# A fused add and layer norm on one core: other chunk sizes, lags and store queues for the last chunks

## Chip, core and metric

The kernel runs on one core of a Trainium2 chip. The metric is the time of one execution on the device in microseconds (us); the span of a profile is the time from the first to the last instruction on the core and is some 2 us shorter than that time.

## What is computed

```python
def reference(x, residual, gamma, beta, eps):      # x, residual: 16 x 1024 x 512 float32
    z = x + residual
    mean = np.mean(z, axis=-1, keepdims=True)
    var = np.var(z, axis=-1, keepdims=True)
    z_norm = (z - mean) / np.sqrt(var + eps)
    return (gamma * z_norm + beta).astype(np.float32)
```

There are 16,384 rows of 512 numbers. Each row is read twice (from `x` and from `residual`) and written once: 67 MB in, 34 MB out.

## The kernel before

The rows are cut into 128 *units* of 128 rows, one row per partition of the on-chip memory. A *chunk* is one or more units that are loaded with one transfer for `x` (tile `z`), one for `residual` (tile `r`), and stored with one. `_chunk_schedule` (line 16) makes the list of chunk sizes: two chunks of 1, then chunks of 4 as long as they fit (29 of them), a remainder of 2, and eight chunks of 1 at the end: 40 chunks.

What happens to a chunk, stage by stage:

- `s_load` (line 119): SyncE issues both loads (lines 128 and 131). For each unit TensorE multiplies `z` and `r` by the identity and adds both into one bank of its accumulator memory, `ps` (lines 137 and 138): this is the addition `x + residual`.
- `s_copy` (line 159): ScalarE copies `ps` back to `z` and sums each row on the way (line 164).
- `s_square` (line 172): ScalarE squares `z` into a scratch tile `junk` and sums the squares (line 178).
- `s_smalls` (line 185): VectorE makes mean and variance for all units of the chunk from these sums, with three instructions on 128 x (units) numbers (lines 191, 194, 195).
- `s_sqrt` (line 204): ScalarE takes the root of variance + eps (line 208).
- `s_recip` (line 216): VectorE inverts it (line 221) and computes `nbias`, -mean / std (line 222). Nothing in the path that is used here reads `nbias`.
- `s_ap1` (line 254): VectorE computes (z - mean) * gamma, one instruction of 128 x 512 for each unit (line 258).
- `s_ap2_store` (line 267): VectorE computes that times 1/std plus beta, again one instruction for each unit (line 271); then GpSimd issues the store of the whole chunk (line 279).

The tiles `z` and `r` have ten buffers each, every one as large as the largest chunk; `ps` has eight.

The stages of a chunk are emitted with lags. In iteration `i` of the loop at line 307, a stage with lag `l` is emitted for chunk `i - l`; the lags are 0 for the load, 1 for copy and square, 2 for the small statistics and the root, 3 for the reciprocal and for `s_ap1`, and 4 for `s_ap2_store`:

```python
    for i in range(n_chunks + max_lag):
        for lag, fn in stages:
            c = i - lag
            if 0 <= c < n_chunks:
                fn(c)
```

The kernel is written in a tile framework, which places all semaphore waits and, when the context closes, fixes the order of the instructions on each engine. The emission order gives the priority; it need not be the final order. That order is fixed before the run[...].

Of the kernel before, what the change touches and what calls it, by code (L numbers as in the profile page):

```python
# [2 lines left out]

# [5 lines left out]


def _env(name, default):
    return int(os.environ.get(name, str(default)))


def _chunk_schedule(total_units, body_nj, head, tail):
    head = [h for h in head if h > 0]
    tail = [t for t in tail if t > 0]
    njs = []
    left = total_units - sum(head) - sum(tail)  # L20
    assert left >= 0
    njs += head
    n_body = left // body_nj
    njs += [body_nj] * n_body
    rem = left - n_body * body_nj
    if rem:
        njs += [rem]
    njs += tail
    assert sum(njs) == total_units
    return njs  # L30
# [3 lines left out]
def kernel(  # L34
# [6 lines left out]
    eps: bass.AP,  # L41
    out: bass.AP,
):
    USE_PE = _env("LN_PE", 1)
    NJ = _env("LN_NJ", 4)
    N_HEAD = _env("LN_HEAD", 2)
    N_TAIL = _env("LN_TAIL", 8)
    Z_BUFS = _env("LN_BUFS", 10)
    R_BUFS = _env("LN_RBUFS", 10)
    ST_BUFS = _env("LN_STBUFS", 8)  # L50
    PS_BUFS = _env("LN_PSBUFS", 8)
    OUT_Q = _env("LN_OUT_Q", 2)
    IN_Q = _env("LN_IN_Q", 0)
    L_CP = _env("LN_L_CP", 1)
    L_SQ = _env("LN_L_SQ", 1)
    L_SM = _env("LN_L_SM", 2)
    L_SQR = _env("LN_L_SQR", 2)
    L_RC = _env("LN_L_RC", 3)
    L_AF = _env("LN_L_AF", 3)
    L_GB = _env("LN_L_GB", 4)  # L60

    nc = tc.nc
    fp32 = mybir.dt.float32
# [11 lines left out]
    eps_f = float(eps)  # L75
    inv_d = 1.0 / float(D)

    assert N % P == 0
    total_units = N // P
    njs = _chunk_schedule(total_units, NJ, [1] * N_HEAD, [1] * N_TAIL)  # L80
    n_chunks = len(njs)
    starts = []
    row = 0
# [5 lines left out]
    def dview(t, c):  # L89
        nj = njs[c]  # L90
        return t[starts[c] : starts[c] + P * nj, :].rearrange(
            "(p j) d -> p (j d)", p=P
        )
# [2 lines left out]
    data = ctx.enter_context(tc.tile_pool(name="data", bufs=Z_BUFS))  # L96
    rpool = ctx.enter_context(tc.tile_pool(name="rpool", bufs=R_BUFS))
    stats = ctx.enter_context(tc.tile_pool(name="stats", bufs=ST_BUFS))
    if USE_PE:
        psum = ctx.enter_context(tc.tile_pool(name="psum", bufs=PS_BUFS, space=bass.MemoryType.PSUM))  # L100
        junkp = ctx.enter_context(tc.tile_pool(name="junkp", bufs=2))

    gamma_t = consts.tile([P, D], fp32)
    nc.gpsimd.dma_start(out=gamma_t, in_=gamma[None, :].to_broadcast((P, D)))  # L104
# [1 line left out]
    nc.gpsimd.dma_start(out=beta_t, in_=beta[None, :].to_broadcast((P, D)))  # L106
    eps_t = consts.tile([P, 1], fp32)
    nc.vector.memset(eps_t, eps_f)  # L108
    if USE_PE:
        ident = consts.tile([P, P], fp32)  # L110
        make_identity(nc, ident)
        junk = junkp.tile([P, D], fp32)

    in_q = {0: nc.sync, 1: nc.scalar, 2: nc.gpsimd}[IN_Q]
    out_q = {0: nc.sync, 1: nc.scalar, 2: nc.gpsimd}[OUT_Q]

    Z, R, PS, SUM, SSQ, MEAN, VAR, RSTD, NBIAS = {}, {}, {}, {}, {}, {}, {}, {}, {}

    def s_load(c):
        nj = njs[c]  # L120
        z = data.tile([P, NJB, D], fp32, tag="z")
        r = rpool.tile([P, NJB, D], fp32, tag="r")
        Z[c], R[c] = z, r
        sm = stats.tile([P, NJB], fp32, tag="sum")
        sq = stats.tile([P, NJB], fp32, tag="ssq")
        SUM[c], SSQ[c] = sm, sq
        if USE_PE:
            nc.sync.dma_start(  # L128
                out=z[:, :nj, :].rearrange("p a b -> p (a b)"), in_=dview(xf, c)
            )  # L130
            in_q.dma_start(  # L131
                out=r[:, :nj, :].rearrange("p a b -> p (a b)"), in_=dview(rf, c)
            )
            pss = []
            for j in range(nj):
                ps = psum.tile([P, D], fp32, tag="ps", name="ps")
                nc.tensor.matmul(ps, ident, z[:, j, :], start=True, stop=False)  # L137
                nc.tensor.matmul(ps, ident, r[:, j, :], start=False, stop=True)  # L138
                pss.append(ps)
            PS[c] = pss  # L140
        else:
            nc.sync.dma_start(
                out=z[:, :nj, :].rearrange("p a b -> p (a b)"), in_=dview(xf, c)
            )
            in_q.dma_start(
                out=r[:, :nj, :].rearrange("p a b -> p (a b)"), in_=dview(rf, c)
            )
            for j in range(nj):
                nc.vector.scalar_tensor_tensor(
                    out=z[:, j, :],  # L150
                    in0=z[:, j, :],
                    scalar=0.0,
                    in1=r[:, j, :],
                    op0=add,
                    op1=add,
                    accum_out=sm[:, j : j + 1],
                )

    def s_copy(c):
        nj = njs[c]  # L160
        z = Z[c]
        sm = SUM[c]
        for j in range(nj):
            nc.scalar.activation(  # L164
                out=z[:, j, :],
                in_=PS[c][j],
                func=mybir.ActivationFunctionType.Identity,
                accum_out=sm[:, j : j + 1],
            )
        PS.pop(c)  # L170

    def s_square(c):
        nj = njs[c]
        z, r = Z[c], R[c]
        sq = SSQ[c]
        dest = junk if USE_PE else r
        for j in range(nj):
            nc.scalar.activation(  # L178
                out=dest if USE_PE else r[:, j, :],
                in_=z[:, j, :],  # L180
                func=mybir.ActivationFunctionType.Square,
                accum_out=sq[:, j : j + 1],
            )

    def s_smalls(c):
        nj = njs[c]
        mean = stats.tile([P, NJB], fp32, tag="mean")
        var = stats.tile([P, NJB], fp32, tag="var")
        MEAN[c], VAR[c] = mean, var
        msq = var  # L190
        nc.vector.tensor_scalar(  # L191
            out=mean[:, :nj], in0=SUM[c][:, :nj], scalar1=inv_d, scalar2=None, op0=mult
        )
        nc.vector.tensor_mul(msq[:, :nj], mean[:, :nj], mean[:, :nj])  # L194
        nc.vector.scalar_tensor_tensor(  # L195
            out=var[:, :nj],
            in0=SSQ[c][:, :nj],
            scalar=inv_d,
            in1=msq[:, :nj],
            op0=mult,  # L200
            op1=sub,
        )
# [13 lines left out]
    def s_recip(c):  # L216
        nj = njs[c]
        rstd = RSTD[c]
        nbias = stats.tile([P, NJB], fp32, tag="nbias")
        NBIAS[c] = nbias  # L220
        nc.vector.reciprocal(out=rstd[:, :nj], in_=rstd[:, :nj])  # L221
        nc.vector.scalar_tensor_tensor(  # L222
            out=nbias[:, :nj],
            in0=MEAN[c][:, :nj],
            scalar=-1.0,
            in1=rstd[:, :nj],
            op0=mult,
            op1=mult,
        )

    def s_affine(c):
        nj = njs[c]
        z = Z[c]
        rstd, nbias = RSTD[c], NBIAS[c]
        for j in range(nj):
            nc.scalar.activation(
                out=z[:, j, :],
                in_=z[:, j, :],
                func=mybir.ActivationFunctionType.Identity,
                bias=nbias[:, j : j + 1],  # L240
                scale=rstd[:, j : j + 1],
            )

    def s_gb_store(c):
        nj = njs[c]
        z = Z[c]
        zb = z[:, :nj, :]
        nc.vector.tensor_mul(zb, zb, gamma_t[:, None, :].to_broadcast((P, nj, D)))
        nc.vector.tensor_add(zb, zb, beta_t[:, None, :].to_broadcast((P, nj, D)))
        out_q.dma_start(out=dview(of, c), in_=zb.rearrange("p a b -> p (a b)"))  # L250
        for dd in (Z, R, PS, SUM, SSQ, MEAN, VAR, RSTD, NBIAS):
            dd.pop(c, None)

    def s_ap1(c):
        nj = njs[c]
# [11 lines left out]
    def s_ap2_store(c):  # L267
        nj = njs[c]
        z, rstd = Z[c], RSTD[c]
        for j in range(nj):  # L270
            nc.vector.scalar_tensor_tensor(  # L271
                out=z[:, j, :],
                in0=z[:, j, :],
                scalar=rstd[:, j : j + 1],
                in1=beta_t,
                op0=mult,
                op1=add,
            )
        out_q.dma_start(  # L279
            out=dview(of, c),  # L280
            in_=z[:, :nj, :].rearrange("p a b -> p (a b)"),
        )
        for dd in (Z, R, PS, SUM, SSQ, MEAN, VAR, RSTD, NBIAS):
            dd.pop(c, None)

    stages = [(0, s_load)]
    if USE_PE:
        stages += [
            (L_CP, s_copy),
            (L_SQ, s_square),  # L290
            (L_SM, s_smalls),
# [2 lines left out]
            (L_AF, s_ap1),  # L294
            (L_GB, s_ap2_store),
        ]
    else:
        stages += [
            (L_SQ, s_square),
            (L_SM, s_smalls),  # L300
            (L_SQR, s_sqrt),
# [1 line left out]
            (L_AF, s_affine),  # L303
            (L_GB, s_gb_store),
        ]
    max_lag = max(l for l, _ in stages)
    for i in range(n_chunks + max_lag):
        for lag, fn in stages:
            c = i - lag
            if 0 <= c < n_chunks:  # L310
                fn(c)


# [33 lines left out]
```

## Time and profile before

| | |
|---|---|
| time, median of 4 runs | 254.98 us (254.38 to 256.59) |
| span of the profiled run | 252.8 us |
| TensorE matmul busy | 230.8 us (91%), 512 instructions |
| VectorE busy | 190.1 us (75%), 457 instructions |
| ScalarE busy | 191.8 us (76%), 554 instructions |
| GpSimd busy | 23.4 us (9%) |
| moved by DMA | 101.35 MB, mean 401 GB/s |

In the profile, PE is TensorE's matmul part and PEld its weight loading, DVE is VectorE, ACT is ScalarE, POOL is GpSimd and SP is SyncE (SPq its queue of issued transfers). A row of a timeline gives start, duration, engine, line of the kernel, operation, output and input, and in brackets the idle time before it with what ended it. The second part of the page cuts the span into 40 equal slices; each digit is a busy share in tenths. A busy share over the whole span is a mean over stretches with different limits, so the stretch in which the kernel ends has to be looked at by itself.

### The profile page before, as it was taken

The numbers are of one execution on the slowest core, as the hardware profiler recorded it, in microseconds if no ns is written. First come the engines' busy times: TensorE is split into PE (matmuls) and PEld (weight loads), VectorE is DVE, ScalarE is ACT, GpSimd is POOL, SyncE is SP. The second block draws the span as 40 slices with busy tenths as digits, with TensorE's granted clock in tenths as the row PEclk, the third lists the DMA queues.
The fourth block names the chain that finished last, engine by engine and source line by source line (L and its number), as shares of the span: only waits on it lengthen the run. The fifth ranks groups of instructions, "written<-read, shape, count | busy, mean of one in ns | idle before, by whom it ended". The sixth has DMA issues, their size and how long they took to land.

```text
span 252.8 us, 2444 instructions
## 1 busy us (share of the span) xinstructions
PE 230.8 (91%) x512; PEld 97.2 (38%) x512; DVE 190.1 (75%) x457; ACT 191.8 (76%) x554; POOL 23.4 (9%) x48
## 2 busy tenths in 40 slices
PE   4699999999999999899999999999999999999920
PEld 1134444444444443344333344343433443344400
DVE  0142888988888888788777779878777987779991
ACT  2357888888888888878878788787888878789860
POOL 3000000000000000000000000000000000000231
PEclk9959999999999999999999999999999999999985
DMA  6999999999999999999999999999999999999843
GB/s 183 388 428 424 425 421 426 423 426 430 423 428 425 426 428 425 426 425 424 425 428 425 426 425 428 423 425 429 423 425 428 426 428 423 413 406 392 348 162 124
DMA packets 16815, 101.35 MB, mean 401 GB/s; under 512 B 1952, under 2 KB 1952, under 8 KB 5664
## 3 DMA queue, kind: packets, MB, share of 16 engines
q1 hardware_dynamic: 11520, 67.11, 63.9%
q0 software_dynamic: 5280, 34.08, 32.8%
q8 instruction: 4, 0.07, 0.1%
q14 instruction: 11, 0.09, 0.1%
HBM read 67.63 MB, written 33.55 MB: 400 GB/s over the span
## 4 chain that ended last, share of the span: by engine, by line
DMA 78%; PE 13%; issue 4%; POOL 2%; SPq 1%; POOLq 0%
DMA r<-in_residual_dram 76%; PE ps L138 7%; PE ps L137 6%; DMA z<-in_x_dram 2%; POOL out_dram L279 2%; SPq L128 1%; SPq L131 0%; POOLq L342 0%; POOLq L279 0%
## 5 line engine op out<-in xcount | busy, mean ns | idle before, releaser
L138 PE MATMUL ps<-r,ident 128*128 128x512 f32 x256 | 134.9, 609 | 6.0 <-DMA r<-in_residual_dram 6.0
L137 PE MATMUL ps<-z,ident 128*128 128x512 f32 x256 | 134.4, 607 | 5.0 <-DMA z<-in_x_dram 4.9
L164 ACT ACTIVATE z<-ps 128x512 f32<-128x512 f32 x128 | 76.2, 595 | 32.1 <-PE ps L138 30.9
L258 DVE SCALAR_TENSOR_TENSOR z<-z,mean,gamma_t 128x512 f32<-128x512 f32 x128 | 94.3, 742 | 0.0
L271 DVE SCALAR_TENSOR_TENSOR z<-z,std,beta_t 128x512 f32<-128x512 f32 x128 | 88.4, 747 | 0.0
L178 ACT ACTIVATE junk<-z 128x512 f32<-128x512 f32 x128 | 80.8, 631 | 3.9
L138 PEld LDWEIGHTS ps<-r,ident 128*128 128x128 f32 x256 | 47.9, 193 | 76.0 <-issue 52.5
L137 PEld LDWEIGHTS ps<-z,ident 128*128 128x128 f32 x256 | 49.3, 194 | 67.9 <-issue 54.3
L191 DVE TENSOR_SCALAR mean<-sm 128x4 f32<-128x4 f32 (+2 forms) x40 | 6.6, 166 | 52.4 <-ACT z L164 52.4
L279 POOL DMA_DIRECT2D out_dram<-z x40 | 21.5, 536 | 223.9 <-DVE z L271 199.7
L164 ACT ACTIVATION_READ_ACCUMULATOR z<-ps 128x1 f32 x128 | 24.9, 195 | 0.0
L178 ACT ACTIVATION_READ_ACCUMULATOR junk<-z 128x1 f32 x128 | 24.0, 188 | 0.0
L208 ACT ACTIVATE std<-var,eps_t 128x4 f32<-128x4 f32 (+2 forms) x40 | 11.9, 297 | 14.4 <-DVE var L195 14.2
L221 DVE RECIPROCAL std<-std 128x4 f32<-128x4 f32 (+2 forms) x40 | 6.8, 169 | 2.9 <-ACT std L208 2.9
L194 DVE TENSOR_TENSOR var<-mean 128x4 f32<-128x4 f32 (+2 forms) x40 | 6.5, 161 | 1.1
L195 DVE SCALAR_TENSOR_TENSOR var<-sq,var 128x4 f32<-128x4 f32 (+2 forms) x40 | 6.3, 157 | 0.3 <-ACT junk L178 0.3
L222 DVE SCALAR_TENSOR_TENSOR nbias<-mean,std 128x4 f32<-128x4 f32 (+2 forms) x40 | 6.3, 158 | 0.1
L164 ACT ACT_TABLE_LOAD x1 | 1.3, 1283 | 3.4 <-DMA z<-in_x_dram 3.4
L208 ACT ACT_TABLE_LOAD x1 | 1.3, 1283 | 0.0
L104 POOL DMA_DIRECT2D gamma_t<-in_gamma_dram x1 | 0.7, 677 | 0.8 <-POOLq L328 0.8
L108 DVE MEMSET eps_t<- 128x1 f32 x1 | 0.1, 59 | 0.8 <-PEq L328 0.8
L106 POOL DMA_DIRECT2D beta_t<-in_beta_dram x1 | 0.5, 543 | 0.0
(6 smaller groups left out, 0.9 us busy)
## 6 DMA issues: line engine op xcount, KB each, us to landing
z<-in_x_dram SPq DMA_DIRECT2D x29, 1024.0 KB, 29.4
r<-in_residual_dram SPq DMA_DIRECT2D x29, 1024.0 KB, 29.5
out_dram<-z POOLq DMA_DIRECT2D x29, 1024.0 KB, 9.3
z<-in_x_dram SPq DMA_DIRECT2D x10, 256.0 KB, 7.9
r<-in_residual_dram SPq DMA_DIRECT2D x10, 256.0 KB, 8.0
out_dram<-z POOLq DMA_DIRECT2D x10, 256.0 KB, 2.4
z<-in_x_dram SPq DMA_DIRECT2D x1, 512.0 KB, 28.3
r<-in_residual_dram SPq DMA_DIRECT2D x1, 512.0 KB, 24.7
```

Of the source, the lines that this page charges most:

```text
L137: nc.tensor.matmul(ps, ident, z[:, j, :], start=True, stop=False)
L138: nc.tensor.matmul(ps, ident, r[:, j, :], start=False, stop=True)
L164: nc.scalar.activation(out=z[:, j, :], in_=PS[c][j], func=mybir.ActivationFunctionType.Identity, accum_out=sm[:, j : j + 1],)
L178: nc.scalar.activation(out=dest if USE_PE else r[:, j, :], in_=z[:, j, :], func=mybir.ActivationFunctionType.Square, accum_out=sq[:, j : j ...
L191: nc.vector.tensor_scalar(out=mean[:, :nj], in0=SUM[c][:, :nj], scalar1=inv_d, scalar2=None, op0=mult)
L194: nc.vector.tensor_mul(msq[:, :nj], mean[:, :nj], mean[:, :nj])
L195: nc.vector.scalar_tensor_tensor(out=var[:, :nj], in0=SSQ[c][:, :nj], scalar=inv_d, in1=msq[:, :nj], op0=mult, op1=sub,)
L208: nc.scalar.activation(out=std[:, :nj], in_=VAR[c][:, :nj], func=mybir.ActivationFunctionType.Sqrt, bias=eps_t[:, 0:1], scale=1.0,)
L221: nc.vector.reciprocal(out=rstd[:, :nj], in_=rstd[:, :nj])
L258: nc.vector.scalar_tensor_tensor(out=z[:, j, :], in0=z[:, j, :], scalar=mean[:, j : j + 1], in1=gamma_t, op0=sub, op1=mult,)
L271: nc.vector.scalar_tensor_tensor(out=z[:, j, :], in0=z[:, j, :], scalar=rstd[:, j : j + 1], in1=beta_t, op0=mult, op1=add,)
L279: out_q.dma_start(out=dview(of, c), in_=z[:, :nj, :].rearrange("p a b -> p (a b)"),)
```

## The change

Most of the diff tidies: constants in place of environment variables, a test on the row length in place of a flag, a `fast_path` function that always returns false, and `junk` in a pool of one buffer in place of two. Five parts change what runs:

- the chunk sizes: two of 1, 28 of 4, then 2, 2, 2, 2, 2, 2, 1, 1 (38 chunks); the aim is finer work near the end than chunks of 4, with fewer transfers than chunks of 1;
- `nbias` isn't computed any more on this path;
- `s_ap1` gets lag 4, where it had 3, so that both wide VectorE stages are emitted in the same iteration;
- the last six chunks get shorter lags, 3 for both wide stages, so that they are emitted sooner;
- the stores of the last four chunks are issued by SyncE, the others still by GpSimd.

```diff
 def _chunk_schedule(total_units, body_nj, n_head, n_tail):
+    head = [1] * min(n_head, total_units)
+    tail = [2, 2, 2, 2, 2, 2, 1, 1]
+    left = total_units - len(head) - sum(tail)
+    njs = list(head)
+    njs += [body_nj] * (left // body_nj)
...
+    DRAIN_FAST = 6
+    L_CP, L_SQ, L_SM, L_SQR, L_RC, L_AF, L_GB = 1, 1, 2, 2, 3, 4, 4
...
         nc.vector.reciprocal(out=rstd[:, :nj], in_=rstd[:, :nj])
-        nc.vector.scalar_tensor_tensor(
-            out=nbias[:, :nj],
-            in0=MEAN[c][:, :nj],
-            scalar=-1.0,
-            in1=rstd[:, :nj],
-            op0=mult,
-            op1=mult,
-        )
...
-        out_q.dma_start(
-            out=dview(of, c),
-            in_=z[:, :nj, :].rearrange("p a b -> p (a b)"),
+        (nc.sync if c >= n_chunks - 4 else nc.gpsimd).dma_start(
+            out=dview(of, c), in_=z[:, :nj, :].rearrange("p a b -> p (a b)")
         )
...
+        tail_lags = [0, 1, 1, 2, 2, 3, 3, 3]
...
-    max_lag = max(l for l, _ in stages)
-    for i in range(n_chunks + max_lag):
-        for lag, fn in stages:
-            c = i - lag
-            if 0 <= c < n_chunks:
-                fn(c)
+    emit = []
+    for c in range(n_chunks):
+        fast = c >= n_chunks - DRAIN_FAST
+        for si, (lag, _fn) in enumerate(stages):
+            emit.append((c + (tail_lags[si] if fast else lag), si, c))
+    emit.sort()
+    for _lvl, si, c in emit:
+        stages[si][1](c)
```

For chunks with the ordinary lags the sorted list gives the same order as the two loops did: by iteration, then by stage.

More of the change, by code (lines that the diff above doesn't have):

```diff
@@ L2 @@
-import os
 from contextlib import ExitStack
@@ L9, with _chunk_schedule @@
 from concourse.masks import make_identity
[L12 to L27, printed above, removed]
+def _chunk_schedule(total_units, body_nj, n_head, n_tail):
+    head = [1] * min(n_head, total_units)
[3 more added lines that the diff above has]
+    njs += [body_nj] * (left // body_nj)
+    if left % body_nj:
+        njs.append(left % body_nj)
     njs += tail
@@ L43 @@
 ):
[L44 to L60, printed above, removed]
+    NJ = 4
+    N_HEAD = 2
+    N_TAIL = 8
+    DRAIN_FAST = 6
+    Z_BUFS = 10
+    R_BUFS = 10
+    ST_BUFS = 8
+    PS_BUFS = 8
+    L_CP, L_SQ, L_SM, L_SQR, L_RC, L_AF, L_GB = 1, 1, 2, 2, 3, 4, 4
     nc = tc.nc
@@ L76 @@
     inv_d = 1.0 / float(D)
-    assert N % P == 0
+    assert N % P == 0, "row count must be a multiple of the partition count"
+    use_pe = D <= 512
     total_units = N // P
-    njs = _chunk_schedule(total_units, NJ, [1] * N_HEAD, [1] * N_TAIL)
+    njs = _chunk_schedule(total_units, NJ, N_HEAD, N_TAIL)
     n_chunks = len(njs)
@@ L98 @@
     stats = ctx.enter_context(tc.tile_pool(name="stats", bufs=ST_BUFS))
-    if USE_PE:
+    if use_pe:
         psum = ctx.enter_context(tc.tile_pool(name="psum", bufs=PS_BUFS, space=bass.MemoryType.PSUM))
-        junkp = ctx.enter_context(tc.tile_pool(name="junkp", bufs=2))
+        junkp = ctx.enter_context(tc.tile_pool(name="junkp", bufs=1))
     gamma_t = consts.tile([P, D], fp32)
@@ L108 @@
     nc.vector.memset(eps_t, eps_f)
-    if USE_PE:
+    if use_pe:
         ident = consts.tile([P, P], fp32)
@@ L112, with fast_path @@
         junk = junkp.tile([P, D], fp32)
-    in_q = {0: nc.sync, 1: nc.scalar, 2: nc.gpsimd}[IN_Q]
-    out_q = {0: nc.sync, 1: nc.scalar, 2: nc.gpsimd}[OUT_Q]
-    Z, R, PS, SUM, SSQ, MEAN, VAR, RSTD, NBIAS = {}, {}, {}, {}, {}, {}, {}, {}, {}
+    Z, R, PS, SUM, SSQ, MEAN, VAR, RSTD, NBIAS = ({} for _ in range(9))
+    def fast_path(c):
+        return False
     def s_load(c):
@@ L126, in s_load @@
         SUM[c], SSQ[c] = sm, sq
-        if USE_PE:
-            nc.sync.dma_start(
-                out=z[:, :nj, :].rearrange("p a b -> p (a b)"), in_=dview(xf, c)
-            )
-            in_q.dma_start(
-                out=r[:, :nj, :].rearrange("p a b -> p (a b)"), in_=dview(rf, c)
-            )
+        zv = z[:, :nj, :].rearrange("p a b -> p (a b)")
+        rv = r[:, :nj, :].rearrange("p a b -> p (a b)")
+        nc.sync.dma_start(out=zv, in_=dview(xf, c))
+        nc.sync.dma_start(out=rv, in_=dview(rf, c))
+        if use_pe and not fast_path(c):
             pss = []
@@ L141, in s_load @@
         else:
[L142 to L147, printed above, removed]
             for j in range(nj):
@@ L159, in s_copy @@
     def s_copy(c):
+        if fast_path(c):
+            return
         nj = njs[c]
-        z = Z[c]
-        sm = SUM[c]
+        z, sm = Z[c], SUM[c]
         for j in range(nj):
@@ L173, in s_square @@
         nj = njs[c]
-        z, r = Z[c], R[c]
-        sq = SSQ[c]
-        dest = junk if USE_PE else r
+        z, r, sq = Z[c], R[c], SSQ[c]
         for j in range(nj):
             nc.scalar.activation(
-                out=dest if USE_PE else r[:, j, :],
+                out=junk if (use_pe and not fast_path(c)) else r[:, j, :],
                 in_=z[:, j, :],
@@ L189, in s_smalls @@
         MEAN[c], VAR[c] = mean, var
-        msq = var
         nc.vector.tensor_scalar(
@@ L193, in s_smalls @@
         )
-        nc.vector.tensor_mul(msq[:, :nj], mean[:, :nj], mean[:, :nj])
+        nc.vector.tensor_mul(var[:, :nj], mean[:, :nj], mean[:, :nj])
         nc.vector.scalar_tensor_tensor(
@@ L198, in s_smalls @@
             scalar=inv_d,
-            in1=msq[:, :nj],
+            in1=var[:, :nj],
             op0=mult,
@@ L218, in s_recip @@
         rstd = RSTD[c]
-        nbias = stats.tile([P, NJB], fp32, tag="nbias")
-        NBIAS[c] = nbias
         nc.vector.reciprocal(out=rstd[:, :nj], in_=rstd[:, :nj])
-        nc.vector.scalar_tensor_tensor(
-            out=nbias[:, :nj],
-            in0=MEAN[c][:, :nj],
-            scalar=-1.0,
-            in1=rstd[:, :nj],
-            op0=mult,
-            op1=mult,
[L229 to L241, printed above, removed]
-            )
[L244 to L252, printed above, removed]
+        if not use_pe:
+            nbias = stats.tile([P, NJB], fp32, tag="nbias")
+            NBIAS[c] = nbias
+            nc.vector.scalar_tensor_tensor(
+                out=nbias[:, :nj],
+                in0=MEAN[c][:, :nj],
+                scalar=-1.0,
+                in1=rstd[:, :nj],
+                op0=mult,
+                op1=mult,
+            )
     def s_ap1(c):
@@ L284, in s_ap2_store, with s_affine, s_gb_store @@
             dd.pop(c, None)
-    stages = [(0, s_load)]
-    if USE_PE:
-        stages += [
+    def s_affine(c):
+        nj = njs[c]
+        z = Z[c]
+        rstd, nbias = RSTD[c], NBIAS[c]
+        for j in range(nj):
+            nc.scalar.activation(
+                out=z[:, j, :],
+                in_=z[:, j, :],
+                func=mybir.ActivationFunctionType.Identity,
+                bias=nbias[:, j : j + 1],
+                scale=rstd[:, j : j + 1],
+            )
+    def s_gb_store(c):
+        nj = njs[c]
+        zb = Z[c][:, :nj, :]
+        nc.vector.tensor_mul(zb, zb, gamma_t[:, None, :].to_broadcast((P, nj, D)))
+        nc.vector.tensor_add(zb, zb, beta_t[:, None, :].to_broadcast((P, nj, D)))
+        nc.gpsimd.dma_start(out=dview(of, c), in_=zb.rearrange("p a b -> p (a b)"))
+        for dd in (Z, R, PS, SUM, SSQ, MEAN, VAR, RSTD, NBIAS):
+            dd.pop(c, None)
+    if use_pe:
+        stages = [
+            (0, s_load),
             (L_CP, s_copy),
@@ L296 @@
         ]
+        tail_lags = [0, 1, 1, 2, 2, 3, 3, 3]
     else:
-        stages += [
+        stages = [
+            (0, s_load),
             (L_SQ, s_square),
@@ L305 @@
         ]
-    max_lag = max(l for l, _ in stages)
-    for i in range(n_chunks + max_lag):
-        for lag, fn in stages:
-            c = i - lag
-            if 0 <= c < n_chunks:
-                fn(c)
+        tail_lags = [0, 1, 2, 2, 3, 3, 4]
+    emit = []
[6 more added lines that the diff above has]
+        stages[si][1](c)
 _INS = ['x', 'residual', 'gamma', 'beta', 'eps']
```

## The prediction

> **What bounds the kernel now.** I read the slices of the page first, then the stretches, then the timeline of the end. Units are 128 rows; there are 128 of them.
>
> ```profile
> DVE  0142888988888888788777779878777987779991
> DMA  6999999999999999999999999999999999999843
> GB/s 183 388 428 424 425 421 426 423 426 430 423 428 425 426 428 425 426 425 424 425 428 425 426 425 428 423 425 429 423 425 428 426 428 423 413 406 392 348 162 124
> ```
>
> One slice is 6.32 us. For 32 slices the DMA engines are full at about 425 GB/s with VectorE at 7 to 8 tenths; in the last three the rate falls to 348, 162, 124 and VectorE stands at 9, 9, 9. So the body is bound by transfers and the end by something else. The stretches say what.
>
> ```profile
> 100.00:200.00 100.00, 96.01 (x217) 39.96 (x216) 79.55 (x178) 79.72 (x230) 6.93 (x13) 1.00 1.01 426
> 218.00:225.40 7.40, 7.07 (x18) 3.17 (x18) 5.83 (x13) 5.92 (x17) 0.53 (x1) 1.00 1.03 406
> 234.00:242.00 8.00, 7.85 (x19) 3.19 (x17) 8.00 (x33) 6.93 (x22) 2.17 (x4) 1.00 0.78 312
> 242.00:247.60 5.60, 0.00 (x0) 0.00 (x0) 5.56 (x21) 2.26 (x8) 2.10 (x4) 0.69 0.44 168
> ```
>
> The columns are PE, PEld, DVE, ACT, POOL busy, clock, DMA share, GB/s. Until 225 VectorE has slack; from 234 to 247.6 it has none (8.00 of 8.00, 5.56 of 5.60), while DMA is at 0.78 and then 0.44. The timeline of VectorE shows where this begins and ends:
>
> ```profile
> 217.98 0.17 DVE L191 TENSOR_SCALAR mean<-sm 128x4 f32<-128x4 f32 x1 [1.50 <-ACT z L164]
> 218.27 0.75 DVE L258 SCALAR_TENSOR_TENSOR z<-z,mean,gamma_t 128x512 f32<-128x512 f32 x1
> 221.13 2.73 DVE L271 SCALAR_TENSOR_TENSOR z<-z,std,beta_t 128x512 f32<-128x512 f32 x4
> 225.44 0.17 DVE L191 TENSOR_SCALAR mean<-sm 128x4 f32<-128x4 f32 x1 [1.58 <-ACT z L164]
> ...
> 246.80 0.76 DVE L271 SCALAR_TENSOR_TENSOR z<-z,std,beta_t 128x512 f32<-128x512 f32 x1
> 247.12 0.54 POOL L279 DMA_DIRECT2D out_dram<-z  x1 [0.98 <-DVE z L271]
> 247.85 0.54 POOL L279 DMA_DIRECT2D out_dram<-z  x1 [0.19 <-issue]
> ```
>
> Two chunks of four units start at 217.98 and 225.44. After the first, VectorE is done at 223.86 and idles 1.58 us, because the mean of a chunk needs the copies of all four units. From 225.44 it never stops until 247.56. That is the path: a late start by a coarse chunk, then 22.12 us of VectorE for the last 14 units, then the store.
>
> The timeline also shows that the emitted order is not the order on the engine: the first multiply (L258) of a chunk follows its mean (L191) at once, though the loop emits it an iteration later. The builder moves ready work into VectorE's idle time; lags matter only where VectorE is short.
>
> **What the Trainium skill says.** "Perfetto Trace Analysis", Optimization Strategy: the most contended engine can change over time within a kernel, and is to be judged by regime. The trace agrees (DMA share 1.01 from 100 to 200, VectorE 5.56 of 5.60 us at the end). "VectorE: DVE Perf Modes", Rules for kernel authors: keep the number of operations small, since each flushes the pipe. The trace shows a small price for independent ones: 241.90, 241.97, 242.04, 242.10 are starts of four in a row, 0.07 us apart, and 242.10 to 242.76 makes a wide one 0.66. "DMA: Bandwidth & Descriptors", Issuing engines are not separate DMA queues: another issuing engine brings no bandwidth, only issue time. The page agrees so far: SyncE's loads and GpSimd's stores take 63.9 and 32.8% of one set of 16 engines, 96.7% together. Same page, Latency and other measured facts: first byte about 0.6 us for a transfer issued by SyncE against about 1 us by GpSimd. No SyncE store is in this trace.
>
> **The change part by part.**
>
> *Price check.* By these prices the 22.12 us from 225.44 are 28 wide (28 x 0.66 = 18.48) and 10 chunks of 5 small (50 x 0.07 = 3.50): 21.98.
>
> *Chunks.* The last 14 units, before one of 4, one of 2 and eight of 1, become six of 2 and two of 1; units 2 to 113 stay in fours. So the first line of the fence stays at 217.98, and the next mean needs two copies, not four. Units 114 and 115 pass PE by about 217.06 + 4 x 0.86 = 220.5 and their copies end before 222, before VectorE is free at 223.9. The idle 1.58 us go.
>
> *One small operation fewer* (line 222, which nothing uses here): before, 5 per chunk and 11 chunks from 217.98; after, 4 per chunk and 9 chunks. 55 - 36 = 19 x 0.07 = 1.3 us less. In the body the same removal costs and gives nothing: there VectorE has 1.5 us idle in each 7.4, under transfers.
>
> *Sum on VectorE after:* 36 wide x 0.66 = 23.76, 36 small x 0.07 = 2.52, 0.3 for the first dependent pair (217.98 to 218.19 instead of 0.07) and the last one's full length: 26.6, to 244.6 instead of 247.56.
>
> *Other floors.* PE: at 217.06 two matmuls of 0.43 end at 217.92, the next starts at 218.41 because the residual of the 4-unit chunk is late. With half the size it is there: 0.49 earlier, so PE ends at 241.36 instead of 241.85. Then copy 0.70, square 0.78, variance 0.20, root 0.35, reciprocal 0.21, wide 0.75, hand-overs 0.1: 3.1, to 244.5. DMA: the stretches from 218 to 250 sum to 10.4 MB; at 406 GB/s 25.5 us, to 243.5. Do earlier stores starve the loads? A 1 MB store lands in 9.2 us beside loads, thus takes some 114 GB/s, and stores are in flight from 216.8 to 233 before too; the loads keep their pace and end near 235, PE wants the last at 239.6.
>
> *Three floors within 1.1 us* won't be met exactly: I add 0.6, one wait of the root for its variance (0.51 at 238.73) and a hand-over. Bounds 0 and 2.0, the latter if the engines keep strictly the emitted order: then VectorE's two wide operations of unit 126 and two of unit 127 follow the statistics of 127 at 243.6 and end at 246.6. Last wide operation: 245.2.
>
> *Lags.* Line 258's lag 3 to 4: nothing in the body, as the builder moves it; VectorE's idle 1.5 us hide it. The SyncE queue's waits show that buffers don't limit either (one wait of 2.8 us on a store):
>
> ```profile
> SPq L131 <- DMA r<-in_residual_dram: 113.8, 33, 4.6
> SPq L128 <- DMA z<-in_x_dram: 76.6, 31, 4.3
> SPq L128 <- DMA out_dram<-z: 2.8, 1, 2.8
> ```
>
> The shorter lags of the last six chunks are what lets the 0.6 be small; before, two wide operations followed the last reciprocal (246.08, 246.80), after only one need.
>
> *Last four stores from SyncE.* They wait there for VectorE; behind them on SyncE stand only stores, as the last load was issued at 231.8. Cost: a GpSimd store of 256 KB lands in 2.3 us at least, after a hand-over of 0.29. A SyncE transfer of 256 KB: at most 2.6 (the fastest load, beside a second one), at least 1.9 (2.3 less the page's 0.4). I take 0.2 gained, bounds -0.3 and +0.6. From landing to the span's end 2.65 stay.
>
> *Nothing:* one `junk` buffer fewer, constants for environment values, `fast_path`, which is always false.
>
> *Sum:* 247.56 - 245.2 = 2.36, and 0.2: 2.6 us. Span 252.8 to 250.2; the time was 2.2 above the span, so 254.98 - 2.6 = 252.4 us.
>
> **Rivals.**
> A, the forecast, 252.4, chance 0.60.
> B, order on the engines eats it: strict order gives 246.6, a SyncE store at its worst 0.3 more, gain 0.7: 254.3. For it: ScalarE's root waited on VectorE five times after 217 (2.9 us). Against: VectorE lost nothing by that before. 0.22.
> C, no 0.6 and the quickest store: 247.56 - 244.5 + 0.6 = 3.7 gained, 251.3. For: VectorE without a gap for 22 us before. Against: three floors at once. 0.12.
> D, slower: with VectorE short, each of the eight tail chunks waits for ScalarE in turn, as ScalarE waited 0.86 from 218.71 to 219.57 for a variance. 8 x 0.86 = 6.9 on 244.6, to 251.5, 3.9 later than before: 258.7 with the store's 0.2 taken off. Against: in before the chunks of one show no such gap. 0.06.
>
> **How the numbers follow.** A is likeliest. The range reaches down to C's 251.3 and up past B to 254.9. The line for 1% is 252.43, in the middle of A; two of the four times before lie at 254.4, below the median, so I put 0.38 of A under it, with C 0.50. Slower is D, 0.06; the rest, 0.44, is within 1%.
>
> **What would show it.** VectorE should have no gap between the last 4-unit chunk and the end, its last wide operation near 245.2 (less than 245.8 for A, 246.6 for B), PE's end near 241.4, the last store's landing 1.9 to 2.6 us from its issue, the body at 425 GB/s with the last 4-unit mean near 218. Waits of VectorE on ScalarE after 224, or PE waiting for a load after 220, would prove me wrong.

## The result, and the profile after

The changed kernel takes 252.39 us (median of 11 runs, 250.99 to 253.67); the kernel before, run beside it, 255.61 us (15 runs, 254.38 to 257.88). The ratio is 0.9865, with a 95% interval of 0.983 to 0.990: it is faster by 1.0 to 1.7%. The prediction said 252.4 us. The span of the profiled run is 250.1 us, where 252.8 went before.

The slices of the page after, one slice being 6.25 us:

```profile
DVE  0054888889867779877778977777887777799995
DMA  5999999999999999999999999999999999999954
GB/s 172 381 428 421 423 430 427 421 424 428 428 424 426 426 427 427 427 423 423 427 427 424 428 423 426 427 421 431 424 423 428 424 422 421 420 420 416 397 222 168
```

The body is the same, full transfers at some 425 GB/s. The rate now stays at 416 or more until slice 37; before, it had fallen below that three slices earlier. The stretches of the end say the same (columns as in the prediction):

```profile
218.00:225.40 7.40, 7.40 (x18) 3.23 (x17) 6.25 (x16) 6.21 (x21) 0.38 (x1) 1.00 1.02 418
234.00:242.00 8.00, 7.75 (x19) 3.28 (x18) 7.83 (x22) 6.20 (x20) 1.06 (x2) 1.00 0.81 322
242.00:247.20 5.20, 0.88 (x3) 0.05 (x1) 5.03 (x16) 2.91 (x10) 0.00 (x0) 1.00 0.36 145
```

VectorE is still the engine that is nearly full to the end (7.83 of 8.00, 5.03 of 5.20). The timeline of VectorE and of SyncE's queue, from the last mean of a chunk of four:

```profile
219.11 0.17 DVE L165 TENSOR_SCALAR mean<-sm 128x4 f32<-128x4 f32 x1 [1.56 <-ACT z L141]
222.19 0.75 DVE L223 SCALAR_TENSOR_TENSOR z<-z,std,beta_t 128x512 f32<-128x512 f32 x1
222.85 0.17 DVE L165 TENSOR_SCALAR mean<-sm 128x2 f32<-128x2 f32 x1
...
246.41 0.75 DVE L223 SCALAR_TENSOR_TENSOR z<-z,std,beta_t 128x512 f32<-128x512 f32 x1
240.41 7.12 SPq L231 DMA_DIRECT2D out_dram<-z  x4
```

The first mean of a chunk of two (222.85) slips in between the wide operations of the chunk of four, so VectorE has no gap there. Its last wide operation ends at 247.16, only 0.4 us earlier than before (247.56), and the span ends 2.94 us after it, where it took 5.24.

The absolute positions mislead here. The mean of units 110 to 113 (the first line of this fence; 217.98 before) lies anywhere from 217.97 to 219.11 in twelve profiles of this study, with every edit of the end, so this is taken as a spread of the body and not as an effect of the change. Counted from that mean, call it M, the times add up:

| from the profiles, us | before | after |
|---|---|---|
| M to the end of VectorE's last wide operation | 29.58 | 28.05 |
| from there to the end of the span | 5.24 | 2.94 |
| sum | 34.82 | 30.99 |

That is 3.8 us less (the medians of the times differ by 3.2): 1.5 from VectorE and 2.3 from what follows it. The forecast had 2.4 and 0.2.

### The profile page after: what moved, and what is told of

It is laid out like the page before. It is cut to its first block, busy times and chain, and to the rows that moved or that the text cites. A ratio compares the mean times of both kernels' runs of the same rounds, so it can differ in the third digit from the quotient of the medians.

```text
span 250.1 us, 2385 instructions
## 1 busy us (share of the span) xinstructions
PE 230.3 (92%) x512; PEld 95.9 (38%) x512; DVE 187.6 (75%) x409; ACT 191.9 (77%) x552; POOL 20.0 (8%) x42
## 4 chain that ended last, share of the span: by engine, by line
DMA 44%; issue 40%; DVE 7%; POOL 3%; PE 1%; ACT 1%; SPq 0%; POOLq 0%
DMA z<-in_x_dram 41%; DMA out_dram<-z 4%; DVE z L223 3%; POOL out_dram L231 3%; DVE z L210 3%; PE ps L119 1%; PE ps L120 1%; ACT L182 1%; DVE var L169 0%; ACT junk L153 0%; DVE std L193 0%; ACT z L141 0%; POOLq L231 0%; DVE mean L165 0%; SPq L113 0%
## 5 line engine op out<-in xcount | busy, mean ns | idle before, releaser
L119 PE MATMUL ps<-z,ident 128*128 128x512 f32 x256 | 132.9, 601 | 5.3 <-DMA z<-in_x_dram 5.3
L210 DVE SCALAR_TENSOR_TENSOR z<-z,mean,gamma_t 128x512 f32<-128x512 f32 x128 | 92.2, 742 | 0.0
L120 PEld LDWEIGHTS ps<-r,ident 128*128 128x128 f32 x256 | 47.2, 192 | 78.2 <-issue 49.5
L231 POOL DMA_DIRECT2D out_dram<-z x34 | 18.1, 533 | 216.8 <-DVE z L223 185.0
L182 ACT ACTIVATE std<-var,eps_t 128x4 f32<-128x4 f32 (+2 forms) x38 | 11.2, 296 | 14.3 <-DVE var L169 14.2
```

The costliest lines, as they stand in the source:

```text
L182: nc.scalar.activation(out=std[:, :nj], in_=VAR[c][:, :nj], func=mybir.ActivationFunctionType.Sqrt, bias=eps_t[:, 0:1], scale=1.0,)
L210: nc.vector.scalar_tensor_tensor(out=z[:, j, :], in0=z[:, j, :], scalar=mean[:, j : j + 1], in1=gamma_t, op0=sub, op1=mult,)
L231: (nc.sync if c >= n_chunks - 4 else nc.gpsimd).dma_start(out=dview(of, c), in_=z[:, :nj, :].rearrange("p a b -> p (a b)"))
```

## The experiments

Ratios are to the kernel before, run beside each, with 95% intervals. "M to the last wide operation" is the time from M to the end of VectorE's last wide operation, in the profile of that run.

**The store queue alone.** The kernel before, with

```diff
-        out_q.dma_start(
+        (nc.sync if c >= n_chunks - 4 else out_q).dma_start(
```

> The kernel before with one edit: the stores of its last four chunks (256 KB each) are issued by SyncE. By the prediction's theory (a store from SyncE gains 0.2 us, VectorE is what counts) the time is 0.2 us below before, ratio 0.999, and VectorE's last wide operation to the span's end stays at 5.0 us (5.24 in the trace of before). By the rival formed from the trace after (there it is 2.94 us) this alone takes 2.3 us off, ratio 0.991, and the profile shows about 3.0 us from the last wide operation to the end.

Measured: 0.990 (0.986 to 0.993), 252.92 us. M to the last wide operation 29.19, then 3.26 to the end. The term that the prediction put at 0.2 us is worth 2 us by itself. The 29.19 is 0.39 below the 29.58 of before with the same work on VectorE: its idle time ahead of the second chunk of four was 1.19 us here and 1.58 there. So this figure can differ by some tenths from profile to profile.

**The store queue undone.** The changed kernel with all stores from GpSimd:

```diff
-        (nc.sync if c >= n_chunks - 4 else nc.gpsimd).dma_start(
+        nc.gpsimd.dma_start(
```

> The changed kernel with all stores issued by GpSimd again. By the prediction's theory it keeps nearly all of the gain: 2.4 us below before, ratio 0.991. By the rival it loses 2.3 us against the changed kernel and keeps about 1.0 to 1.5 us, ratio 0.994 to 0.996, with some 5.2 us from VectorE's last wide operation to the end.

Measured: 0.991 (0.988 to 0.995), 253.31 us. M to the last wide operation 28.10, then 5.06. By the profile's parts this is the rival: the 2.1 us after VectorE are gone, VectorE's 1.5 stay. By the ratio alone the two theories can't be told apart, as the interval holds the 0.991 of the first and reaches to the rival's range.

**The last store alone back on GpSimd.** The changed kernel with

```diff
-        (nc.sync if c >= n_chunks - 4 else nc.gpsimd).dma_start(
+        (nc.sync if n_chunks - 4 <= c < n_chunks - 1 else nc.gpsimd).dma_start(
```

> The changed kernel with only its very last store (256 KB) issued by GpSimd, the three ahead of it by SyncE. If the 2.3 us come from the issue and landing of that one transfer (hand-over 0.3, landing 0.3) the loss against the changed kernel is 0.6 us and from landing to the span's end it stays at 0.9 us. If GpSimd's late store also lengthens what comes after the landing (2.6 us in the trace of before, 0.9 after) the loss is the whole 2.3 us.

Measured: 0.994 (0.992 to 0.996), 253.91 us; 4.91 us from VectorE to the end. One store of 256 KB costs 2.0 of the 2.3 us. What happens on GpSimd's queue when the program closes shows why: each engine has closing instructions called DRAIN there. Kernel before, changed kernel, and this one, each with the shortest, median and longest duration in ns and the first and last start in us (in all three the first is the longest):

```profile
L342 POOLq DRAIN  x3: 45/102/4195, 247.8 to 252.5; - x3
```
```profile
L321 POOLq DRAIN  x3: 45/93/6149, 237.4 to 249.9; - x3
```
```profile
L321 POOLq DRAIN  x3: 45/102/3875, 246.5 to 250.8; - x3
```

Before, a DRAIN of 4.2 us starts when GpSimd has taken its last store, at 247.8, and so ends at 252.0; the span ends 0.8 us later. In the changed kernel the DRAIN starts at 237.4 and is over at 243.6, while VectorE still works; SyncE's last store lands 2.0 us after its issue, and the span ends 0.9 us after that. In the third it lasts from 246.5 to 250.3, and the span ends at 251.1.

**Only the very last store on SyncE.**

```diff
-        (nc.sync if c >= n_chunks - 4 else nc.gpsimd).dma_start(
+        (nc.sync if c >= n_chunks - 1 else nc.gpsimd).dma_start(
```

> The changed kernel with only its very last store (256 KB) from SyncE; the store of the chunk ahead is then GpSimd's last, issued some 0.9 us earlier. If the price is GpSimd's closing DRAIN (4.0 us from the issue of its last store, and 0.75 us after it to the span's end), the DRAIN still ends last: 0.9 us earlier than with all stores on GpSimd, so the span ends 3.9 to 4.2 us after VectorE's last wide operation (5.06 with all on GpSimd, 2.94 with four on SyncE). If only the issue and landing of the last store matter, it is 2.94 as in the changed kernel.

Measured: 0.993 (0.990 to 0.997), 253.57 us; 4.19 us from VectorE to the end.

```profile
245.55 0.54 POOL L231 DMA_DIRECT2D out_dram<-z  x1 [2.13 <-DVE std L193]
246.14 0.34 SPq L231 DMA_DIRECT2D out_dram<-z  x1
```
```profile
L321 POOLq DRAIN  x3: 45/93/3967, 245.5 to 250.0; - x3
```

GpSimd's last store goes out at 245.55, its DRAIN of 3.97 ends at 249.5, and the span ends 0.8 later, at 250.3, though the last transfer was SyncE's. So the end is set by the later of two things, GpSimd's DRAIN and the last landing. Moving one store isn't enough; GpSimd's last one has to be issued early enough for the DRAIN to lie behind other work.

**A quarter of the last store on GpSimd.**

```diff
+        if c == n_chunks - 1:
+            nc.gpsimd.dma_start(out=dview(of, c)[:, 384:512], in_=z[:, 0, 384:512])
+            nc.sync.dma_start(out=dview(of, c)[:, 0:384], in_=z[:, 0, 0:384])
...
```

> The changed kernel with the last store split: columns 0 to 383 (192 KB) from SyncE, columns 384 to 511 (64 KB, a quarter) from GpSimd. With the whole 256 KB on GpSimd, its closing DRAIN lasted 3.9 us from the store's issue and ended 0.7 us ahead of the span's end; with SyncE alone GpSimd's DRAIN was over at 243.6 and the span ended 2.94 us after VectorE. If the DRAIN waits for the bytes of the store, a quarter of them takes some 0.5 us less (256 KB moved in 0.6 to 0.8 us): DRAIN 3.4 us. If it is a fixed price of any late store from GpSimd, it stays at 3.9 and the span ends 4.9 us after VectorE's last wide operation, as with the whole store.

Measured: 0.994 (0.990 to 0.997), 253.23 us; 4.72 us from VectorE to the end, DRAIN 3.66 us. With 256 KB as the last GpSimd store the DRAIN took 3.88 to 4.27 in seven profiles. A quarter of the bytes takes a few tenths off, so the price is neither fixed nor proportional to the bytes. Set beside the landing of GpSimd's last store, the DRAINs fall into line:

| GpSimd's last store, us | lands after its issue | DRAIN takes |
|---|---|---|
| this run, 64 KB | 2.05 | 3.66 |
| last store alone on GpSimd, 256 KB | 2.30 | 3.88 |
| kernel before, 256 KB | 2.42 | 4.20 |
| changed kernel, 512 KB | 4.62 | 6.15 |
| longer tail with 14 buffers (below), 512 KB | 6.56 | 8.14 |

In all fourteen profiles the DRAIN ends 1.5 to 1.8 us after that landing. In the changed kernel it ends at 243.6, though SyncE's stores land until 249.24, so it goes with GpSimd's own stores. No run delays a landing by itself, and what takes the 1.5 us is left open.

**The chunk sizes alone.** The kernel before, with the last 14 units as in the changed one:

```diff
-    njs = _chunk_schedule(total_units, NJ, [1] * N_HEAD, [1] * N_TAIL)
+    njs = _chunk_schedule(total_units, NJ, [1] * N_HEAD, [2, 2, 2, 2, 2, 2, 1, 1])
```

> The kernel before with one edit: the last 14 units as chunks of 2, 2, 2, 2, 2, 2, 1, 1. Both theories: VectorE has no gap between the last chunk of four and the end, so its time from the mean of the last chunk of four to its last wide operation's end falls from 29.6 us (before) by the idle 1.6 us, plus 10 small operations fewer at 0.07, to about 27.3 by the prediction's price of 0.07 for each small one; if small ones that wait for the one ahead cost 0.20, as in the trace after, to about 28.5. The end after it stays at 5.2 us. Time 1.0 to 2.3 us below before, ratio 0.991 to 0.996.

Measured: 0.996 (0.994 to 0.999), 253.75 us. M to the last wide operation 28.22 (29.58 before), then 5.09. The sizes bring 1.4 of VectorE's 1.5 us. Where the forecast's other 0.8 went is seen in the changed kernel's timeline, where nothing independent stands between two dependent operations:

```profile
233.89 0.16 DVE L165 TENSOR_SCALAR mean<-sm 128x2 f32<-128x2 f32 x1
234.09 0.16 DVE L168 TENSOR_TENSOR var<-mean 128x2 f32<-128x2 f32 x1
...
235.57 0.16 DVE L193 RECIPROCAL std<-std 128x2 f32<-128x2 f32 x1
235.76 1.41 DVE L223 SCALAR_TENSOR_TENSOR z<-z,std,beta_t 128x512 f32<-128x512 f32 x2
237.09 0.16 DVE L165 TENSOR_SCALAR mean<-sm 128x2 f32<-128x2 f32 x1
```

From the mean to the variance's start 0.20 us pass, from the reciprocal to the wide operation 0.19; independent ones followed each other 0.07 apart. A chunk of two takes 3.20 us (233.89 to 237.09) where the forecast had 4 x 0.66 + 4 x 0.07 = 2.92.

**Line 222 alone removed.** The kernel before, with

```diff
-        nbias = stats.tile([P, NJB], fp32, tag="nbias")
-        NBIAS[c] = nbias
         nc.vector.reciprocal(out=rstd[:, :nj], in_=rstd[:, :nj])
-        nc.vector.scalar_tensor_tensor(
-            out=nbias[:, :nj],
...
-        )
```

> The kernel before without line 222 (the mean over std that nothing reads). By the prediction's price, 0.07 us for each of the 11 small operations after the mean of units 110 to 113, VectorE's stretch from that mean to its last wide operation's end falls from 29.6 by 0.8 us, time ratio 0.997. By the rival (another small operation's place only turns into a wait of the next wide one for the reciprocal) it falls by 0.3 us at most, ratio 0.999 to 1.000.

Measured: 0.999 (0.997 to 1.002), 254.38 us. In the profile M to the last wide operation is 28.82, 0.76 less than before, so the price of 0.07 for each held where chunks of one gave VectorE independent neighbours; in time it isn't told from nothing. With the new chunk sizes the same removal is worth 0.12 (28.22 with sizes alone, 28.10 with all but the queue), no more than such figures scatter. There a small operation less uncovers a wait: with the sizes alone, 7 of 45 small operations after M are followed by the next start only after some 0.2 us, in the changed kernel 12 of 36.

**The lags undone.** The changed kernel with

```diff
-    DRAIN_FAST = 6
+    DRAIN_FAST = 0
-    L_CP, L_SQ, L_SM, L_SQR, L_RC, L_AF, L_GB = 1, 1, 2, 2, 3, 4, 4
+    L_CP, L_SQ, L_SM, L_SQR, L_RC, L_AF, L_GB = 1, 1, 2, 2, 3, 3, 4
```

> The changed kernel with the lags of before (line 258's stage at 3, no shorter lags for the last chunks). The order on TensorE, ScalarE, GpSimd and SyncE is then the same as in the changed kernel, and on VectorE it differs in a dozen rows around two chunks only. Prediction's theory: the shorter lags keep the drain short; without them some 0.7 us is lost, one wide operation. Rival: the lags do nothing, ratio to the changed kernel 1.000, VectorE's stretch from the mean of units 110 to 113 stays at 28.1 us.

Measured: 0.987 (0.983 to 0.990), 251.09 us; M to the last wide operation 28.04, then 2.97. The lags do nothing that shows: the rows of TensorE, ScalarE, GpSimd and SyncE come in the same order as in the changed kernel, and on VectorE only a few differ.

**A longer fine tail.** Eight chunks of 2 and two of 1:

```diff
-    tail = [2, 2, 2, 2, 2, 2, 1, 1]
+    tail = [2] * 8 + [1, 1]
```

> The changed kernel with a tail of eight chunks of 2 and two of 1 (18 units instead of 14, chunks of 4 until unit 109). If VectorE's late start behind chunks of 4 is what sets its end, starting it four units earlier lets it catch up with TensorE: its last wide operation ends 3.1 us after TensorE's last matmul (4.3 in the trace after), and the time falls by another 1.0 us, ratio to before 0.982 to 0.984. If TensorE or the loads set the end already, nothing changes (ratio 0.986).

Measured: 1.003 (1.001 to 1.005), 256.12 us: slower than before. Its timeline of TensorE and VectorE:

```profile
234.01 1.02 PE L120 MATMUL ps<-r,ident 128*128 128x512 f32 x2
238.28 1.72 PE L119 MATMUL ps<-z,ident 128*128 128x512 f32 x2 [3.24 <-DMA z<-in_x_dram]
...
244.40 0.17 DVE L165 TENSOR_SCALAR mean<-sm 128x2 f32<-128x2 f32 x1 [5.31 <-ACT z L141]
```

VectorE did catch up, then stood 5.31 us behind TensorE, which waited for a `z` load, the one issued at 220.24:

```profile
212.72 0.33 SPq L113 DMA_DIRECT2D z<-in_x_dram  x1
213.99 5.29 SPq L114 DMA_DIRECT2D r<-in_residual_dram  x3
220.24 0.33 SPq L113 DMA_DIRECT2D z<-in_x_dram  x1
221.50 0.33 SPq L114 DMA_DIRECT2D r<-in_residual_dram  x1
```

Until then `z` and `r` loads alternate. Here three residual loads stand in a row, and two of them would follow this `z` load in the usual order. A chunk of two takes a whole buffer of four, and a `z` load may start only after the store of the chunk ten earlier: ten buffers are then 20 units ahead instead of 40. But SyncE didn't wait for that store, which had landed at 210.46. It waited for earlier loads: eight loads were in flight, and each of these was issued 0.06 to 0.08 us after one had landed. So what the buffers change is the order of the loads, which is fixed before the run.

**The same with 14 buffers for `z`.**

```diff
-    tail = [2, 2, 2, 2, 2, 2, 1, 1]
+    tail = [2] * 8 + [1, 1]
-    Z_BUFS = 10
+    Z_BUFS = 14
```

> The tail of eight chunks of 2 and two of 1 again, now with 14 buffers for z in place of 10 (a chunk of 2 takes a whole buffer of 4). The longer tail was slower: TensorE waited 3.2 us for a z load near the end, and the last z loads stood behind residual loads of later chunks, since each waits for the store of the chunk ten earlier. If buffers are the cause, the wait goes, VectorE's last wide operation comes 3.1 us after TensorE's end, and the ratio to before is 0.982 to 0.984. If the earlier stores take the transfers' time from the loads, the wait stays and the ratio is 1.000 to 1.003 as with 10 buffers.

Measured: 0.992 (0.989 to 0.995), 253.50 us. All loads alternate and the wait for `z` is gone, so the buffers were most of the loss, 2.9 us by the two ratios; but TensorE now waits twice for a residual load:

```profile
233.64 1.13 PE L120 MATMUL ps<-r,ident 128*128 128x512 f32 x2 [0.53 <-DMA r<-in_residual_dram]
237.82 1.13 PE L120 MATMUL ps<-r,ident 128*128 128x512 f32 x2 [0.48 <-DMA r<-in_residual_dram]
```

and VectorE twice for ScalarE (0.39 and 0.89). Neither theory fits alone. Why these loads are late is not shown. One reading is that the stores start earlier while the transfers are full. Another is that eight loads in flight are half the bytes once the chunks are half as large. No run separates them.

**14 buffers with the changed kernel's tail.**

```diff
-    Z_BUFS = 10
+    Z_BUFS = 14
```

> The changed kernel with 14 buffers for z in place of 10, nothing else. In its trace TensorE waits 0.25 to 0.4 us for the last z load. If buffers matter only in the longer tail, this is the changed kernel: ratio to before 0.986 to 0.987, TensorE's wait gone, VectorE's stretch 28.0 us as before, since VectorE is behind TensorE anyway. If the loads' lateness did set the end, it gains up to 0.4 us, ratio 0.985.

Measured: 0.984 (0.980 to 0.988), 250.98 us, which overlaps the changed kernel's interval. TensorE's wait for the last `z` load (0.25 to 0.58 us in the profiles with ten buffers) is gone, its end comes 23.3 us after M in place of 23.8, and M to the end of the span is 31.02, as in the changed kernel (30.99). So a TensorE that ends 0.5 us sooner doesn't bring VectorE's end forward, and no gain is shown.

**Work moved from VectorE to GpSimd.** The changed kernel with 14 buffers, and for two units of its last chunk of four, which VectorE leaves out,

```diff
+            nc.gpsimd.tensor_scalar(
+                out=zj, in0=zj, scalar1=MEAN[c][:, j : j + 1], scalar2=rstd[:, j : j + 1],
+                op0=sub, op1=mult,
+            )
+            nc.gpsimd.tensor_mul(zj, zj, gamma_t)
+            nc.gpsimd.tensor_add(zj, zj, beta_t)
...
```

> The changed kernel with 14 buffers for z, and two of the four units of its last chunk of 4 finished by GpSimd (three instructions of 128 x 512 for each unit) in place of VectorE, which so has four wide operations fewer, 4 x 0.66 = 2.6 us. If VectorE sets the end, its stretch from the mean of units 110 to 113 falls from 28.0 until TensorE's end plus 3.1 us stops it: in the profile with 14 buffers TensorE ended 23.3 us after that mean, so to 26.4, and the ratio to before goes from 0.984 to 0.978. If TensorE, ScalarE or the loads set the end, the stretch stays at 28.0. GpSimd's later store of that chunk should cost nothing, as its last store still lies 9 us ahead of the end.

Measured: 1.000 (0.998 to 1.003), 254.88 us; M to the last wide operation 31.7, 3.6 more than without. The expectation failed on a cost that it hadn't counted:

```profile
225.30 2.49 POOL L231 TENSOR_TENSOR z<-z,gamma_t 128x512 f32<-128x512 f32 x2
227.75 2.94 POOL L232 TENSOR_TENSOR z<-z,beta_t 128x512 f32<-128x512 f32 x2
```
```profile
225.38 1.20 DVE L171 TENSOR_TENSOR var<-mean 128x2 f32<-128x2 f32 x1
226.50 1.83 DVE L213 SCALAR_TENSOR_TENSOR z<-z,mean,gamma_t 128x512 f32<-128x512 f32 x1
228.26 1.22 DVE L172 SCALAR_TENSOR_TENSOR var<-sq,var 128x2 f32<-128x2 f32 x1
229.41 1.83 DVE L213 SCALAR_TENSOR_TENSOR z<-z,mean,gamma_t 128x512 f32<-128x512 f32 x1
```

While GpSimd runs its two-input operations, VectorE's wide ones take 1.83 us in place of 0.75 and its small ones 1.2 in place of 0.16. For the question at hand the run still serves: TensorE ended at 241.24, no later than elsewhere, VectorE ended at 249.66, and the whole span moved with VectorE. So VectorE has no slack against the end. That less work on VectorE would end the kernel sooner, this run does not show.

## Why the prediction was right, and where only its sum was

- *The bound.* Right. VectorE sets the end. It waits for no other engine after the last chunk of four; delayed by 3.6 us with TensorE in time, it took the end along.
- *The idle 1.58 us go.* Right: the sizes alone bring 1.4 us on VectorE.
- *Sum on VectorE, and 0.6 on top.* The sum had 26.6 us from M, 27.2 with the 0.6; measured 28.05. The step that failed is the single price of 0.07 us for every small operation but one. In the changed kernel 12 of the 36 have a dependent neighbour and cost some 0.2; eleven more than forecast, at 0.13 each, are 1.4 us, the whole difference from 26.6. The root's wait, for which the 0.6 was meant, did not reach VectorE: it has no wait for ScalarE after M.
- *Line 222.* 0.76 us on VectorE in the old sizes against 0.8 forecast for 11 of them, but 0.12 in the new ones. The sum of 1.3 us counted line 222 and the fewer chunks as if both came off in full.
- *Other floors.* TensorE's end was forecast 23.4 us after M and came at 23.8, as the last `z` load was late. "The loads keep their pace and end near 235" was wrong: the last one landed at 240.79 and TensorE still waited for it, 0.25 us until 240.93. The prediction had named such a wait as a sign against itself. It did no harm, since VectorE was behind TensorE: with 14 buffers the wait was gone and nothing was gained.
- *Lags.* That a higher lag for line 258 does nothing was right. That the shorter ones of the last chunks keep the rest small was wrong: without them M to the last wide operation is 28.04.
- *Stores from SyncE.* The step that failed most: "From landing to the span's end 2.65 stay." They don't: it was 2.54 us before and is 0.90 now. In the kernel before, GpSimd's DRAIN ended 1.76 us after the landing of its last store and the span 0.78 after that; with SyncE last, that DRAIN is long over. The transfer's own part was 0.64 us (hand-over 0.29 to 0.02, landing 2.42 to 2.05), where 0.2 was forecast with 0.6 as the upper bound. The term was worth 2.3 us, not 0.2. The Trainium skill, "DMA: Bandwidth & Descriptors" (section "Latency and other measured facts"), was used for a first byte 0.4 us earlier from SyncE; lone stores of 256 KB landed 0.3 us apart (2.3 and 2.0), which fits, but it wasn't the price that counted. What the prediction took from the same page, that another issuing engine saves only issue time, doesn't hold for these last stores: the change of engine was worth 2.3 us, 1.6 of them after the landing.
- *Buffers don't limit.* Right for this tail, by a small margin: with four units more in chunks of two, ten buffers cost 2.9 us. The waits of 113.8 and 76.6 us in the prediction's fence are SyncE's waits for earlier loads, with eight in flight; they were passed over.
- *Readings of the page.* The three 9s of VectorE are slices 37 to 39, with 392, 348 and 162 GB/s; in slice 40 (124) it stands at 1, and the rate begins to fall in slice 35. In D, ScalarE's wait for the variance was 0.42 us, and most of the rest of the 0.86 is the root itself. The 2.2 us between time and span set the median of four runs beside the span of one; that run took 254.62, 1.8 above its span. None of these changes the forecast's gain.

The mechanism was right in one half, VectorE and the coarse chunk, and wrong in the other, what follows VectorE. That the time of 252.4 was met is luck in its parts: a gain of 2.4 us came to 1.5 and one of 0.2 us came to 2.3. Their sum, 3.8 us, is above the 2.6 forecast; the medians differ by 3.2, and the kernel before took 255.61 us beside the changed one, where the forecast had started from 254.98.

## What to carry to other kernels

When a kernel's end matters, look at what each queue does after its last instruction, and not at the last transfer alone: a wait that no busy row shows can be the last link. Here the last store of the engine with the slow close had to go out early enough for its DRAIN to lie behind other work, and with full transfers that DRAIN took up to 8.1 us. Price a small operation by whether it has an independent neighbour; 0.07 and 0.20 us are different prices for the same row. Finer chunks at the end use up buffers, and a longer fine tail was slower here with ten buffers (1.003) and with 14 (0.992 against 0.984), so it isn't the finer the better.

## What the hardware showed that was not expected

- GpSimd's DRAIN at the end of the program took 3.7 us (after a last store of 64 KB) to 8.1 us (512 KB beside other transfers), counted from that store's issue, and ended 1.5 to 1.8 us after its landing in all fourteen profiles. SyncE's DRAINs took 7 ns, and where SyncE's store landed last and GpSimd's DRAIN was over, the span ended 0.9 to 1.3 us after the landing (seven profiles).
- In no profile were more than eight of SyncE's loads in flight; 67 to 70 of the 76 to 80 were issued with seven others on their way. What sets this number is not shown.
- A two-input operation of GpSimd on 128 x 512 float32 slowed VectorE's operations to 1.83 us from 0.75, small ones to 1.2 from 0.16. GpSimd's one-input operation (5.39 us for two, 219.94 to 225.3) left most of them at their usual 0.75; whether GpSimd itself was held up then, no run shows. The Trainium skill, "SBUF — State Buffer" (section "Who interferes with whom"), says that a VectorE instruction with two inputs in SBUF contends with a GpSimd instruction that reads SBUF, as its second input comes through a read interface that the two share. The trace agrees for the two-input operations, and not for the one-input one, which also reads SBUF.
